# The last doubling level of a delta rule on one 64x64 block per head, with a longer latency in the scheduler for one small gather

## The chip, the core and the metric

The program runs on one core of a Trainium2 chip. The metric is device time in microseconds (us) of one execution. TensorE (PE in the profile, with PEld for its weight loads) does the matmuls and the transposes, VectorE (DVE), ScalarE (ACT) and GpSimd (POOL) the elementwise work, and SyncE (SP) issues nearly all DMAs. Each engine works through its own list of instructions in order and waits on semaphores for the others.

## The reference, cut to what matters

Two transformer blocks follow each other. The first mixes its 1024 tokens with a retention and with a gated delta rule of 4 heads, then runs a mixture of experts; the second has neighbourhood attention, a gated linear attention and an MLP. The change lies in the delta rule of the first block. With `C` the chunk length, it solves a unit lower triangular system in each chunk and carries a state from chunk to chunk:

```
a_mat = where(tri_strict, (k_beta @ k.T) * decay, 0)
t_mat = triangular_solve(eye + a_mat, eye, lower=True, unit_diagonal=True)
u = t_mat @ v_beta;  w = t_mat @ (k_beta * exp(g))
def step(state, inp):
    v_new = u_n - w_n @ state
    o_n = qg_n @ state + attn_n @ v_new
    state = state * gl_n + kt_n.T @ v_new
```

The kernel uses chunks of 128 tokens, so there are 8 of them, each with 4 heads and a 128x128 triangular matrix per head.

## The kernel before

**How work is ordered.** The program records every instruction as an object (all through one helper, which is why nearly every row of the profile names line 347), gives it a cost and a latency by a table, and then lists the instructions engine by engine: of those that are ready, the one with the largest sum of costs to the end of the program goes first. `load.lat`, which the change touches, is an addition to such an estimate; it alters no instruction, only the places where instructions stand.

**The delta rule.** `dn_pre(n)` makes, for chunk n, the matrix `dN` (the reference's `a_mat`, chunk rows on the partitions), its companions, and stores them (tensors `nb_d` and `pre_d`). `dn_blocks(s)` loads the 16x16 diagonal blocks of four chunks from `nb_d` into tile `N` (runs of 64 bytes), inverts them with 15 pairs of small VectorE steps, and stores the result to `xb_d`. `dn_scan(n)` builds the inverse of the whole matrix of a chunk by doubling: `Uf` holds the transposed inverse, `Ti` the inverse, first with 16x16 blocks only. At a level of block size b, GpSimd multiplies `dN` by a mask that keeps the blocks of size b under the diagonal (`AM`), four matmuls give `pp = AM.T @ Uf`, ScalarE copies that to `P`, four matmuls give `pu = Ti.T @ P`, VectorE subtracts it from `Uf`, and, but for the last level, four transposes and a VectorE copy make the new `Ti`. Levels are b = 16, 32, 64. Then the chunk's outputs and the state follow: a chain of matmuls with `vb`, `S` and `vn`. `mix_d` takes the result.

**What runs beside it.** `dn_chunks` records pre 0 to 3, blocks 0, scan 0, pre 4 and 5, scan 1, pre 6 and 7, blocks 1, scans 2 to 7. The scans are serial through the state. Between them on TensorE stand the filler, namely the projections of `tok_blocks` (128x512 matmuls in fp32r, a form of fp32 that takes one pass; each big product is three such), and the `retention` of the same tokens, 8 serial chunks whose single buffers make the load of one chunk wait for the end of the one before. After all this comes `mix_out`, from which on the order is the same in both kernels. A plain fp32 matmul of 128x128 shows as two TensorE records in the trace, a transpose as one.

The lines that matter: N's load (L1132), the VectorE steps (L1138 to L1144), the mask product (L1195), `pp` (L1199), the copy to `P` (L1201), `pu` (L1204), the subtraction (L1205), the transposes (L1209).

Of the kernel before, what the change touches and what calls it, by code (L numbers as in the profile page):

```python
# [15 lines left out]
AF = mybir.ActivationFunctionType  # L16
# [497 lines left out]
def shape_constants():  # L514
    i = np.arange(128)
    g = Cols()
    g.add('ident', np.eye(128))
    g.add('ones', np.ones((128, 128)))
    a = Cols()
    a.add('triU', i[:, None] <= i[None, :])  # L520
    a.add('bigN', BIG * (i[None, :] >= i[:, None]))
    a.add('negT', -BIG * (i[None, :] < i[:, None]))
    a.add('blk', i[:, None] // 16 == i[None, :] // 16)
    for b in (16, 32, 64):
        same = (i[:, None] // (2 * b)) == (i[None, :] // (2 * b))
        a.add(f'm{b}', same & ((i[:, None] // b) % 2 == 1) & ((i[None, :] // b) % 2 == 0))
    gam = 1.0 - 2.0 ** (-5.0 - np.arange(4.0))
    a.add('gq', gam[None, :] ** (i[:, None] + 1.0))
    a.add('gk', gam[None, :] ** (127.0 - i[:, None]) * 128.0 ** -0.5)
    a.add('rmask', (gam ** -128.0)[None, :, None] * (i[None, None, :] >= i[:, None, None]))  # L530
    a.add('invf', 10000.0 ** (-np.arange(0, 128, 2) / 128.0))
    m = Cols()
    m.add('strictU', i[:, None] < i[None, :])
    m.add('iota128', np.arange(128.0))
    m.add('iota64', np.arange(32.0) - 64.0)
    e32 = np.arange(32.0)
    kofs = -e32 - 2.0 ** 17 * (e32 < Kern.NS)
    m.add('kofs', np.concatenate([np.tile(kofs, (128, 1)), np.tile(kofs, 4)[:, None]], 1))
    m.add('ecol', np.tile(e32, 4)[:, None])
    m.add('iotaB', np.where(np.kron(np.eye(4), np.ones((32, 32))) > 0, np.tile(e32, 4), -1.0))  # L540
    m.add('tok', i[:, None] + 128.0 * np.arange(8)[None, :])
    w = Cols()
    cq, ck = i[:, None] % 64, np.arange(64)[None, :]
    cs = np.clip(cq - 8, 0, 48)
    w.add('colmask', np.where((ck >= cs) & (ck < cs + 16), 0.0, -BIG))
    l = Cols()
    l.add('m64', (i[:, None] % 64) > np.arange(64)[None, :])
    return {'k_g': g, 'k_a': a, 'k_m': m, 'k_n': w, 'k_l': l}, gam
# [14 lines left out]
class Kern:  # L563
# [564 lines left out]
    def dn_blocks(self, s):  # L1128

        nc, pd, V = self.nc, self.pd, self.nc.vector  # L1130
        N = self.t(pd, [128, 512], tag='P', bufs=2)[:, 0:256].rearrange("p (i j) -> p i j", j=16)
        nc.sync.dma_start(N, self.dram_ap(self.nb_d, 128 * 2064 * s, [[2064, 128], [128, 16], [1, 16]]))  # L1132
        X = self.t(pd, [128, 16, 2, 16], tag='AM', bufs=2)
        Y = self.t(pd, [128, 512], tag='P', bufs=2)[:, 0:256].rearrange("p (i j) -> p i j", j=16)
        flat = X.rearrange("p i t j -> p (i t j)")
        V.memset(flat, 0.0)
        V.memset(flat[:, 0:512:33], 1.0)
        for i in range(15):  # L1138
            r = [128, 15 - i, i + 1]
            y, x = Y[:, i + 1:, 0:i + 1], X[:, i + 1:, 0, 0:i + 1]  # L1140
            V.tensor_tensor(out=y, in0=N[:, i + 1:, i:i + 1].to_broadcast(r),
                            in1=X[:, i:i + 1, 0, 0:i + 1].to_broadcast(r), op=OP.mult)
            V.tensor_tensor(out=x, in0=x, in1=y, op=OP.subtract)
        V.tensor_copy(X[:, :, 1], X[:, :, 0].rearrange("p i j -> p j i"))  # L1144
        nc.sync.dma_start(self.xb_d[128 * s:128 * s + 128], flat)

    def dn_scan(self, A, n):
        nc, pd, sc = self.nc, self.pd, self.sc
        mm, tr = nc.tensor.matmul, nc.tensor.transpose
# [13 lines left out]
        kh, khT, dN, dT = [W[:, i] for i in range(4)]  # L1163
# [3 lines left out]
        Uf = self.t(pd, [128, 4, 128], tag='U', bufs=2)  # L1167
        Ti = self.t(pd, [128, 4, 128], tag='Ti', bufs=2)
        blk = A['blk'].rearrange("p (k j) -> p k j", j=16)[:, None].to_broadcast([128, 4, 8, 16])
        for eng, t, x in ((nc.gpsimd, 1, Uf), (nc.vector, 0, Ti)):  # L1170
            eng.tensor_tensor(out=x.rearrange("p h (k j) -> p h k j", j=16), in1=blk,
                              in0=C[:, :, t:t + 1, :].to_broadcast([128, 4, 8, 16]), op=OP.mult)
        for b in (16, 32, 64):
            AM = self.t(pd, [128, 4, 128], tag='AM', bufs=2)
            nc.gpsimd.tensor_tensor(out=AM, in0=dN, in1=A[f'm{b}'][:, None, :].to_broadcast([128, 4, 128]),
                                    op=OP.mult)
            pp = self.ps([128, 4, 128], 'dn')
            for h in range(4):
                mm(pp[:, h, :], AM[:, h, :], Uf[:, h, :], start=True, stop=True)
            P = self.t(pd, [128, 4, 128], tag='P', bufs=2)  # L1180
            nc.scalar.activation(P, pp, AF.Copy)
            pu = self.ps([128, 4, 128], 'dn')
            for h in range(4):
                mm(pu[:, h, :], Ti[:, h, :], P[:, h, :], start=True, stop=True)
            nc.vector.tensor_tensor(out=Uf, in0=Uf, in1=pu, op=OP.subtract)
            if b < 64:
                pt = self.ps([128, 4, 128], 'dn')
                for h in range(4):
                    tr(pt[:, h, :], Uf[:, h, :], self.ident)
                nc.vector.tensor_copy(Ti, pt)  # L1190
        pv = self.ps([128, 4, 128], 'tp')
        for h in range(4):
            tr(pv[:, h, :], lv_[:, h, :], self.ident)
# [1422 lines left out]
```

## Time and profile before

| | us |
|---|---|
| time, median of 3 runs | 2712.98 (2708.91 to 2715.82) |
| time of the profiled execution | 2710.75 |
| its span in the trace | 2708.9 |
| TensorE busy in it | 2529.4 (93%) |
| VectorE, ScalarE, GpSimd busy | 1801.0, 1194.9, 689.4 |

The span is what the trace covers; some 2 us of the time lie around it. Times of rows below are us from the span's start. The delta rule lies between about 190 and 612 us; all that the change reorders is between 190 and 640 us.

### The profile page before, as it was taken

The page shows a single profiled execution, that of the slowest core. Times are in us where ns is not written, and L with a number is a line of the kernel's source. Part 1 is how long each engine was busy: PE and PEld are TensorE (multiplying, and loading weights), DVE is VectorE, ACT ScalarE, POOL GpSimd, SP SyncE. Part 2 cuts the span into 40 slices and gives each one's busy share as a digit, 9 for nine tenths or more (in the row PEclk, how much of TensorE's full clock was granted, in tenths as well). Part 3 has the DMA queues.
Part 4 walks back from the last instruction along what each step waited for, and adds up shares of the span by engine and source line. Part 5 has one row for each costly group of instructions (what it writes and reads, how often), then busy time and mean ns, then how long its engine had stood idle before and what let it go on. Part 6 is the DMA issues. An engine that isn't in the chain of part 4 may idle for free. (4 is left out here: it accounts for less than half of the span.)

```text
span 2708.9 us, 35429 instructions
## 1 busy us (share of the span) xinstructions
PE 2529.4 (93%) x12278; PEld 1924.6 (71%) x12278; DVE 1801.0 (66%) x2583; ACT 1194.9 (44%) x2005; POOL 689.4 (25%) x703
## 2 busy tenths in 40 slices
PE   5999999999969999999996999999999999999998
PEld 4787777886657766454444777777787888887876
DVE  8557865546679889786776344358736767578874
ACT  5234332332236677565554434247714334453332
POOL 3006541422451111322234201144213003310002
PEclk9999999999979999999998999999999999999999
DMA  7238586565349999999978442263244768787473
GB/s 254 79 118 235 175 249 189 167 205 198 133 170 340 342 347 337 351 320 364 354 263 304 138 125 92 75 195 91 69 133 162 233 221 297 282 288 239 145 249 129
DMA packets 342100, 586.30 MB, mean 216 GB/s; under 512 B 74970, under 2 KB 112526, under 8 KB 338846
## 3 DMA queue, kind: packets, MB, share of 16 engines
q1 hardware_dynamic: 335262, 567.22, 62.6%
q0 software_dynamic: 6656, 16.79, 1.8%
q8 instruction: 97, 1.59, 0.2%
q14 instruction: 85, 0.70, 0.1%
HBM read 477.40 MB, written 112.41 MB: 218 GB/s over the span
## 5 line engine op out<-in xcount | busy, mean ns | idle before, releaser
L347 PE MATMUL psum_all<-sbuf 128*128 128x512 f32 (+10 forms) x12278 | 2529.4, 366 | 167.7 <-DVE sbuf L347 102.5
L347 PEld LDWEIGHTS psum_all<-sbuf 128*128 128x128 f32 (+6 forms) x12278 | 1924.6, 176 | 772.0 <-issue 158.9
L347 ACT ACTIVATE sbuf<-sbuf 128x1024 fp32r<-128x1024 f32 (+9 forms) x894 | 816.1, 937 | 769.9 <-PE psum_all L347 355.6
L347 DVE TENSOR_TENSOR sbuf<-sbuf,sbuf 128x1024 fp32r<-128x1024 f32 (+1 forms) x592 | 725.9, 1251 | 216.0 <-ACT sbuf L347 207.5
L347 ACT ACTIVATE sbuf<-psum_all 128x512 f32<-128x512 f32 (+12 forms) x742 | 345.9, 477 | 688.8 <-PE psum_all L347 636.6
L347 POOL TENSOR_TENSOR sbuf<-sbuf 128x512 f32<-128x512 f32 (+8 forms) x353 | 446.1, 1273 | 761.2 <-DVE sbuf L347 361.4
L347 DVE TENSOR_TENSOR sbuf<-sbuf 128x1024 f32<-128x1024 f32 (+12 forms) x417 | 316.4, 778 | 108.3 <-ACT sbuf L347 31.5
L347 DVE TENSOR_TENSOR sbuf<-psum_all,sbuf 128x512 f32<-128x512 f32 (+12 forms) x290 | 171.5, 603 | 157.7 <-ACT sbuf L347 71.4
L347 DVE SCALAR_TENSOR_TENSOR sbuf<-sbuf 128x512 f32<-128x512 f32 (+5 forms) x263 | 209.3, 803 | 46.3 <-POOL sbuf L347 36.9
L347 POOL TENSOR_SCALAR sbuf<-sbuf 128x1 f32<-128x1 f32 (+3 forms) x182 | 79.7, 440 | 627.0 <-ACT sbuf L347 491.9
L347 DVE TENSOR_TENSOR sbuf<-sbuf,psum_all 128x512 f32<-128x512 f32 (+6 forms) x191 | 123.5, 663 | 118.0 <-PE psum_all L347 112.7
L347 DVE TENSOR_SCALAR sbuf<-sbuf 128x32 f32<-128x32 f32 (+7 forms) x220 | 109.5, 510 | 60.9 <-ACT sbuf L347 42.0
L1809 POOL DMA_INDIRECT y_d<-sbuf x35 | 57.4, 1641 | 195.8 <-DVE sbuf L347 194.5
L347 DVE SCALAR_TENSOR_TENSOR sbuf<-sbuf,psum_all 128x128 f32<-128x128 f32 (+1 forms) x100 | 38.2, 411 | 84.9 <-PE psum_all L347 54.1
L1797 POOL DMA_INDIRECT sbuf<-h_d,sbuf x35 | 45.1, 1288 | 186.0 <-PE psum_all L347 153.1
L347 DVE SCALAR_TENSOR_TENSOR sbuf<-psum_all,sbuf 128x128 f32<-128x128 f32 (+9 forms) x109 | 62.0, 586 | 37.9 <-PE psum_all L347 37.4
L347 POOL MEMSET sbuf<- 64x64 f32 (+10 forms) x54 | 16.9, 314 | 193.4 <-DVE sbuf L347 114.9
L347 DVE CUSTOM_DVE_ANT_0 sbuf<-psum_all,sbuf 128x512 f32<-128x512 f32 (+2 forms) x80 | 48.1, 613 | 22.3 <-PE psum_all L347 21.8
L347 POOL TENSOR_TENSOR sbuf<-sbuf,sbuf 128x1024 fp32r<-128x1024 f32 x16 | 40.9, 2561 | 40.2 <-ACT sbuf L347 39.3
L347 ACT ACTIVATE sbuf<-psum_all,sbuf 128x128 f32<-128x128 f32 (+1 forms) x72 | 24.4, 402 | 35.5 <-PE psum_all L347 23.0
L347 DVE COPY sbuf<-psum_all 128x512 f32<-128x512 f32 (+9 forms) x39 | 20.6, 528 | 22.2 <-PE psum_all L347 19.0
L347 ACT ACTIVATION_READ_ACCUMULATOR sbuf<-sbuf 128x1 f32 x152 | 28.9, 190 | 0.0
(18 smaller groups left out, 112.3 us busy)
## 6 DMA issues: line engine op xcount, KB each, us to landing
sbuf<-in_w SPq DMA_DIRECT2D x384, 512.0 KB
sbuf<-in_w_ff SPq DMA_DIRECT2D x120, 512.0 KB
sbuf<-u_d SPq DMA_DIRECT2D x64, 512.0 KB
sbuf<-in_w_in SPq DMA_DIRECT2D x56, 512.0 KB
sbuf<-in_w_ada SPq DMA_DIRECT2D x48, 512.0 KB
u_d<-sbuf SPq DMA_DIRECT2D x64, 256.0 KB
sbuf<-in_x SPq DMA_DIRECT2D x16, 512.0 KB
sbuf<-qkv_d SPq DMA_DIRECT2D x32, 256.0 KB
```

The source lines that it names most:

```text
L347: op = self.new_op(eng, lambda: real(*a, **k), name, reads, writes)
L1797: return self.prog.real.gpsimd.indirect_dma_start(out=xg, out_offset=None, in_=self.h2_d, in_offset=bass.IndirectOffsetOnAxis(ap=tok, axis=0),
L1809: st = self.prog.real.gpsimd.indirect_dma_start(out=self.y_d, out_offset=bass.IndirectOffsetOnAxis(ap=dest, axis=0), in_=y, in_offset=None ...
```

## The change

It does the last level, b = 64, on the only block that this level has: rows 64 to 127 by columns 0 to 63 of each head. The mask `m64` and its product go. `pp` and `pu` become 64x64 matmuls that read 64 partitions (of `dN` directly, without mask), `P` and `Uf` are written only in that block, and as `Uf` is zero there before, the subtraction becomes a copy with factor -1 on ScalarE. And the load of `N` counts as 8000 ns longer in the scheduler's estimate.

```diff
-    for b in (16, 32, 64):
+    for b in (16, 32):
...
...
-        nc.sync.dma_start(N, self.dram_ap(self.nb_d, ...))
+        load = nc.sync.dma_start(N, self.dram_ap(self.nb_d, ...))
+        load.lat += 8000.0
...
-        for b in (16, 32, 64):
+        for b in (16, 32):
             AM = ...; pp = ...; P = ...; pu = ...
             nc.vector.tensor_tensor(out=Uf, in0=Uf, in1=pu, op=OP.subtract)
-            if b < 64:
-                pt = self.ps([128, 4, 128], 'dn')
-                for h in range(4):
-                    tr(pt[:, h, :], Uf[:, h, :], self.ident)
-                nc.vector.tensor_copy(Ti, pt)
+            pt = self.ps([128, 4, 128], 'dn')
+            for h in range(4):
+                tr(pt[:, h, :], Uf[:, h, :], self.ident)
+            nc.vector.tensor_copy(Ti, pt)
+
+        lo, up = slice(0, 64), slice(64, 128)
+        pp = self.ps([64, 4, 64], 'dn')
+        for h in range(4):
+            mm(pp[:, h, :], dN[up, h, lo], Uf[up, h, up], start=True, stop=True)
+        P = self.t(pd, [128, 4, 128], tag='P', bufs=2)
+        nc.scalar.activation(P[lo, :, lo], pp, AF.Copy)
+        pu = self.ps([64, 4, 64], 'dn')
+        for h in range(4):
+            mm(pu[:, h, :], Ti[lo, h, lo], P[lo, h, lo], start=True, stop=True)
+        nc.scalar.activation(Uf[lo, :, up], pu, AF.Copy, scale=-1.0)
```

In each of the 8 scans this takes away one GpSimd product of 128x512, eight fp32 matmuls of 128x128, one ScalarE copy of 128x512 and one VectorE subtraction of 128x512, and adds eight fp32 matmuls of 64x64 and two ScalarE copies of 64x256. The numbers of transposes and copies to `Ti` stay.

**TensorE, the last level of scan 6.** The rows are TensorE's in order; 128x128 are the delta rule's and the retention's matmuls and transposes, 128x512 the filler, and 64x64 the new matmuls. Before:

```order
L347 MATMUL psum_all<-sbuf_61 128x128 x4
L347 MATMUL psum_all<-sbuf_62 128x512
L347 MATMUL psum_all<-sbuf_61 128x128 x20
L347 MATMUL psum_all<-sbuf_62 128x512
L347 MATMUL psum_all<-sbuf_61 128x128 x8
L347 MATMUL psum_all<-sbuf_62 128x512 x5
```

The same place in the changed kernel:

```order
L347 MATMUL psum_all<-sbuf_62 128x512 x2
L347 MATMUL psum_all<-sbuf_61 64x64
L347 MATMUL psum_all<-sbuf_61 128x128
L347 MATMUL psum_all<-sbuf_61 64x64
L347 MATMUL psum_all<-sbuf_61 128x128 x2
L347 MATMUL psum_all<-sbuf_61 64x64
L347 MATMUL psum_all<-sbuf_61 128x128
L347 MATMUL psum_all<-sbuf_61 64x64
L347 MATMUL psum_all<-sbuf_62 128x512 x5
L347 MATMUL psum_all<-sbuf_61 64x64
```

The four `pp` no longer stand among matmuls of their own size; each is a single 64x64 between two of 128x128, here the transposes of the level before, which become ready at the same moment. Over the whole program the 64 new matmuls stand in 61 separate places: one group of four, and 60 single ones.

**VectorE, around the second `dn_blocks`.** Rows `128x15` and `128x14x2` are the first steps of the block inverse, `128x1024` are splits of weights for the filler, and `TENSOR_SCALAR` and `SCALAR_TENSOR_TENSOR` of 128x512 a product of the modulation vector. Before:

```order
L347 TENSOR_TENSOR sbuf_61<-psum_all,sbuf_61 128x512 x4
L347 TENSOR_TENSOR sbuf_62<-sbuf_61,sbuf_62 128x1024
L347 TENSOR_TENSOR sbuf_61<-sbuf_61 128x15
L347 TENSOR_TENSOR sbuf_62<-sbuf_61,sbuf_62 128x1024
L347 TENSOR_TENSOR sbuf_61<-sbuf_61 128x15
L347 TENSOR_TENSOR sbuf_62<-sbuf_61,sbuf_62 128x1024
L347 TENSOR_TENSOR sbuf_61<-sbuf_61 128x14x2 x2
```

Changed:

```order
L347 TENSOR_TENSOR sbuf_61<-psum_all,sbuf_61 128x512 x4
L347 TENSOR_TENSOR sbuf_62<-sbuf_61,sbuf_62 128x1024 x3
L347 TENSOR_TENSOR sbuf_61<-psum_all,sbuf_61 1x512
L347 TENSOR_SCALAR sbuf_61<-sbuf_61 128x512
L347 SCALAR_TENSOR_TENSOR sbuf_61<-sbuf_61 128x512
L347 SCALAR_TENSOR_TENSOR sbuf_61<-sbuf_61,psum_all 128x512
L347 SCALAR_TENSOR_TENSOR sbuf_61<-sbuf_61 128x512 x2
L347 TENSOR_TENSOR sbuf_61<-sbuf_61 128x15
L347 SCALAR_TENSOR_TENSOR sbuf_61<-sbuf_61 128x512
```

The first step moves behind the three weight splits and behind part of a modulation product, and the other 30 steps with it. On SyncE the store to `xb_d` follows: it stands 24 rows behind the load of `N` where it stood 17 behind it.

**TensorE, the end of the stage.** The long row of 128x512 is the filler between the last two chunks of the retention; 128x24 and 128x36 set up `mix_out`. Before:

```order
L347 MATMUL psum_all<-sbuf_61 128x128 x12
L347 MATMUL psum_all<-sbuf_62 128x512 x54
L347 MATMUL psum_all<-sbuf_61 128x128 x4
L347 MATMUL psum_all<-sbuf_62 128x512 x5
L347 MATMUL psum_all<-sbuf_61 128x128 x4
```

Changed:

```order
L347 MATMUL psum_all<-sbuf_61 128x128 x12
L347 MATMUL psum_all<-sbuf_62 128x512 x24
L347 MATMUL psum_all<-sbuf_61 128x24
L347 MATMUL psum_all<-sbuf_61 128x36 x8
L347 MATMUL psum_all<-sbuf_61 128x128 x28
```

The other filler has gone to earlier places: 24 instead of 54 stand before the last chunk of the retention, and none within it.

## Rows read from the trace of the kernel before

**Rows 1.** The page's first part (busy time and share of the span) and the head of its fourth (the chain of work that ended last, by engine).

```profile
PE 2529.4 (93%) x12278; PEld 1924.6 (71%) x12278; DVE 1801.0 (66%) x2583; ACT 1194.9 (44%) x2005; POOL 689.4 (25%) x703
...
PE 41%; DMA 3%; DVE 2%; issue 1%; POOL 1%; ACT 1%; POOLq 0%; SPq 0%; ACTq 0%; DVEq 0%
```

**Rows 2.** Stretches of the span: length, then busy time and number of records of each engine, the granted TensorE clock, the DMA share and GB/s.

```profile
190.00:263.00 73.00, 67.71 (x360) 54.56 (x358) 53.90 (x84) 39.00 (x121) 39.48 (x42) 1.00 0.78 235
263.00:295.00 32.00, 31.14 (x131) 24.88 (x132) 24.41 (x64) 8.08 (x27) 12.73 (x13) 0.95 0.78 236
295.00:350.00 55.00, 49.74 (x274) 39.73 (x273) 43.80 (x55) 20.44 (x64) 35.15 (x31) 0.97 0.56 177
350.00:405.00 55.00, 50.88 (x303) 43.15 (x304) 32.03 (x53) 20.71 (x66) 21.17 (x22) 1.00 0.81 239
405.00:440.00 35.00, 31.36 (x147) 23.02 (x147) 24.39 (x57) 5.13 (x8) 1.28 (x1) 1.00 0.90 255
440.00:480.00 40.00, 39.16 (x278) 36.59 (x279) 20.88 (x49) 12.52 (x43) 11.60 (x13) 0.96 0.46 141
480.00:520.00 40.00, 38.01 (x265) 34.00 (x264) 23.54 (x40) 13.43 (x32) 15.62 (x15) 1.00 0.50 169
520.00:560.00 40.00, 39.95 (x292) 36.92 (x291) 22.46 (x53) 15.24 (x47) 13.86 (x18) 1.00 0.41 139
560.00:612.00 52.00, 48.12 (x306) 42.13 (x304) 25.01 (x41) 16.44 (x48) 16.46 (x16) 1.00 0.71 237
```

**Rows 3.** TensorE's own timeline, the places where it sat idle before a stretch of work: start, length, the first instruction of the stretch, number of records, and in brackets the idle time before it and what ended that.

```profile
263.86 32.25 PE L347 MATMUL psum_all<-sbuf 128*128 128x128 f32 x135 [3.12 <-ACT sbuf L347]
298.24 4.60 PE L347 MATMUL psum_all<-sbuf 128*128 128x128 f32 x27 [2.13 <-POOL sbuf L347]
327.50 18.01 PE L347 MATMUL psum_all<-sbuf 128*128 128x128 f32 x87 [2.05 <-POOL sbuf L347]
392.05 11.83 PE L347 MATMUL psum_all<-sbuf 128*128 128x128 f32 x65 [2.69 <-DVE sbuf L347]
440.84 69.88 PE L347 MATMUL psum_all<-sbuf 128*128 128x128 f32 x489 [2.92 <-DMA sbuf<-rq_d]
516.10 46.14 PE L347 MATMUL psum_all<-sbuf 128*128 128x128 f32 x332 [0.96 <-DMA sbuf<-rq_d]
600.56 10.37 PE L347 MATMUL psum_all<-sbuf 128*128 128x128 f32 x61 [1.24 <-DMA sbuf<-rq_d]
614.21 2.08 PE L347 MATMUL psum_all<-sbuf 128*128 128x36 f32 x14 [3.28 <-DVE sbuf L347]
617.16 4.10 PE L347 MATMUL psum_all<-sbuf 128*128 128x128 f32 x14 [0.86 <-DVE sbuf L347]
```

**Rows 4.** Two short stretches of TensorE alone: in the first all records are fp32 of 128x128, in the second all are 128x512.

```profile
470.30:478.10 7.80, 7.80 (x72) 1.00 0.52 167
278.00:295.00 17.00, 17.00 (x76) 1.00 0.59 187
```

**Rows 5.** The weight loads' timeline in a later stage of the kernel, where single fp32 matmuls with a stationary tile of 128x64 and of 128x128 follow each other directly, each with two records and 128 columns. Start, length, form and number of records, idle before.

```profile
1730.98 0.19 PEld L347 LDWEIGHTS psum_all<-sbuf 128*64 128x64 f32 x2 [0.35 <-issue]
1731.34 0.20 PEld L347 LDWEIGHTS psum_all<-sbuf 128*128 128x128 f32 x2 [0.17 <-issue]
1731.71 0.63 PEld L347 LDWEIGHTS psum_all<-sbuf 128*64 128x64 f32 x10 [0.17 <-issue]
```

**Rows 6.** The same view elsewhere: four transposes of 64x64, one record each, behind other forms.

```profile
1104.72 0.32 PEld L347 LDWEIGHTS psum_all<-sbuf 64*128 64x128 f32 x4 [0.36 <-issue]
```

**Rows 7.** Groups by form between 440 and 612 us: number, busy time and mean ns of one, idle before and its releasers; the last row, from the same view of the whole span, is a copy of 64x256.

```profile
L347 POOL TENSOR_TENSOR sbuf<-sbuf 128x512 f32<-128x512 f32 x30 | 39.3, 1328 | 72.6 <-PE psum_all L347 53.5 <-DVE sbuf L347 15.4 <-DMA sbuf<-pre_d 3.5
L347 ACT ACTIVATE sbuf<-psum_all 128x512 f32<-128x512 f32 x50 | 29.5, 597 | 80.9 <-PE psum_all L347 80.7
L347 DVE TENSOR_TENSOR sbuf<-sbuf,psum_all 128x512 f32<-128x512 f32 x22 | 15.1, 686 | 30.4 <-PE psum_all L347 30.3
...
L347 ACT ACTIVATE sbuf<-psum_all 64x256 f32<-64x256 f32 x16 | 5.8, 373 | 1.9 <-PE psum_all L347 1.9
```

**Rows 8.** The block inverse on VectorE's timeline: the first steps of `dn_blocks` 0, then the first steps of `dn_blocks` 1, three rows of modulation and weight work near it, and its last copy.

```profile
271.40 2.57 DVE L347 TENSOR_TENSOR sbuf<-sbuf 128x15 f32<-128x15 f32 x11
...
403.43 0.18 DVE L347 TENSOR_TENSOR sbuf<-sbuf 128x15 f32<-128x15 f32 x1
...
416.10 0.68 DVE L347 SCALAR_TENSOR_TENSOR sbuf<-sbuf,psum_all 128x512 f32<-128x512 f32 x1
...
423.44 0.37 DVE L347 COPY sbuf<-sbuf 128x256 f32<-128x256 f32 x1
...
432.82 1.23 DVE L347 TENSOR_TENSOR sbuf<-sbuf,sbuf 128x1024 fp32r<-128x1024 f32 x1 [1.93 <-ACT sbuf L347]
```

**Rows 9.** SyncE's issues (start, length, transfer) around `dn_blocks` 1: the load of `N`, the store to `xb_d`, the next loads of it.

```profile
399.33 0.37 SPq L347 DMA_DIRECT2D sbuf<-nb_d  x1
...
423.96 0.47 SPq L347 DMA_DIRECT2D xb_d<-sbuf  x1
...
428.95 0.92 SPq L347 DMA_DIRECT2D sbuf<-xb_d  x2
```

**Rows 10.** GpSimd's longest wait between 398 and 432 us: waited for, total us, times, longest.

```profile
POOL sbuf L347 <- DMA xb_d<-sbuf: 29.7, 1, 29.7
```

**Rows 11.** SyncE's issues at the end of the stage.

```profile
592.11 0.32 SPq L347 DMA_DIRECT2D zg_d<-sbuf  x1
595.89 0.32 SPq L347 DMA_DIRECT2D sbuf<-mod_d  x1
596.46 0.32 SPq L347 DMA_DIRECT2D sbuf<-rq_d  x1
```

More of the change, by code (lines that the diff above doesn't have):

```diff
@@ L1131, in dn_blocks @@
         N = self.t(pd, [128, 512], tag='P', bufs=2)[:, 0:256].rearrange("p (i j) -> p i j", j=16)
-        nc.sync.dma_start(N, self.dram_ap(self.nb_d, 128 * 2064 * s, [[2064, 128], [128, 16], [1, 16]]))
+        load = nc.sync.dma_start(N, self.dram_ap(self.nb_d, 128 * 2064 * s, [[2064, 128], [128, 16], [1, 16]]))
+        load.lat += 8000.0
         X = self.t(pd, [128, 16, 2, 16], tag='AM', bufs=2)
```

## The prediction, made before the changed kernel ran

> **What bounds the kernel now.** The first part of the page and the chain of waits come first: TensorE is busy for 93% of the span and stands ahead of every other engine in the chain that ended last [rows 1]. Shares over a whole span say nothing of one stage, so the stretches of the stage come next [rows 2]. They show two kinds. From 440 to 560 us TensorE is busy 117.1 of 120 us and VectorE, ScalarE and GpSimd at most 59% of any row: here a microsecond of TensorE work is a microsecond of time. Up to 440 us TensorE idles more, 19 us in 250; and its timeline names who it waited for: GpSimd at 298.24 and 327.50, VectorE at 392.05, the retention's load of q at 440.84 [rows 3]. There, work taken from GpSimd or VectorE can pay, and TensorE work can hide. At the stage's end TensorE waits again, for the load of the retention's last q and then for VectorE [rows 3]. So the question is what the change does to TensorE's own time first, and to these few waits second.
>
> **TensorE work removed.** Eight fp32 matmuls of 128x128 in each of 8 scans, 64 in all, two records each. A stretch of such records alone shows 72 in 7.80 us, of which one is cut by the edge: 0.11 us each [rows 4]. 64 x 2 x 0.11 = 14.1 us go.
>
> **TensorE work added.** 64 fp32 matmuls of 64x64, again two records each. No such matmul is in the trace. Their bare records are bounded by four 64x64 transposes in 0.32 us, 0.08 each [rows 6], and by half of 0.11, since half as many columns stream; I take 0.07, 128 x 0.07 = 9.0 us (7.0 to 10.2). Were that all, TensorE would win 5 us. But the order puts the 64 matmuls in 61 separate places between 128-wide ones, and the trace has that case. Single matmuls with stationary tiles of 128x64 and 128x128 follow each other at 1730.98, 1731.34 and 1731.71, that is 0.36 and 0.37 us each [rows 5], against 2 x 0.11 = 0.22 for two such records in a row. Nothing holds them (the idle before each is marked as issue): a change of the tile's size costs about 0.145 us, on the way in and on the way out. With only 64 columns to finish the way out should be cheaper by half a record, 0.05, so I put 0.24 on each separate place: 61 x 0.24 = 14.6 us. Bounds: 61 x 0.29 = 17.7 us, and nothing, if a 64x64 tile differs from the 128x64 one of those rows. Sum: 9.0 + 14.6 - 14.1 = +9.5 us, between 7.0 - 14.1 = -7.1 and 17.7 + 10.2 - 14.1 = +13.8. Between these ends I stay by the row on alternating tiles, which is the same pattern on the same engine.
>
> The Trainium skill has two rules here that pull apart, both on the page TensorEngine Tiling (Array Packing). Its section Theoretical Speedup gives a matmul with one small dimension up to twice the throughput, and with two small ones more; by that the added 9.0 us would at most be halved or quartered, and with nothing for the separate places the time is that of the second rival below. Its section Key Properties says "Mode switching requires drain", which speaks against the change, since the order switches 122 times; it names no price. The trace agrees with the second, with 0.36 us where 0.22 would do; no run here shows two tiles at work at once.
>
> **The other engines' share of the level.** GpSimd loses one 128x512 product per scan, 8 x 1.33 = 10.6 us, VectorE one subtraction, 8 x 0.69 = 5.5 us; ScalarE exchanges a 0.60 us copy for two of 0.37, 8 x 0.15 = +1.2 us [rows 7]. After 440 us all of this lies beside TensorE, which is the bound, and is worth nothing by itself; the cover is the filler, and where that is gone the chain of one scan gets 0.69 + 0.60 - 2 x 0.37 = 0.55 us shorter. Only scans 0 and 1 run where TensorE waits for GpSimd and VectorE. Their two 1.33 us products may shorten the two waits of 2.13 and 2.05 us, but the order still places other products of the same size ahead, and a TensorE wait at 440.84 is for a load that does not move. The same place hides a part of two scans' added TensorE work, 2/8 of 9.5 = 2.4 us at most. I put -1 us on both together, between -11 (the waits at 298.24, 327.50, 392.05 and 440.84 sum to 9.8, and 1 us of shorter chains) and +2.
>
> **The 8000 ns.** They are a belief of the scheduler, not a wait. The load of N was never late: the first VectorE step of blocks 0 at 271.40 and of blocks 1 at 403.43 have no idle time before them [rows 8]. So nothing is gained there, and the 31 steps stand later. In blocks 1 the first step now stands behind modulation steps that ran until about 416.1, 12.5 us later than 403.43; the end stands behind a split of weights that ran at 432.82, where the last copy had started at 423.44 [rows 8], some 10 us later. Behind that copy is the store to `xb_d` at 423.96 on SyncE, and behind it the loads at 428.95 [rows 9]; behind the loads GpSimd waits, for 29.7 us already [rows 10], and scans 2 to 7. While they wait TensorE does filler, which the order has pulled forward. So the delay costs nothing at once; it costs filler, and the bill comes at the end.
>
> **The end of the stage.** Between retention chunks 6 and 7 lies a round trip of a store and the load of q at 596.46 [rows 11], and chunk 7 starts at 600.56 after 1.24 us of idle [rows 3]. Now 54 matmuls of 128x512 fill it, at 17.00 us for 75, 0.227 each [rows 4], 12.2 us. In the changed order 24 stand there, 5.4 us, and the set-up of `mix_out`, about 2.1 us by the row at 614.21 [rows 3]: 12.2 - 7.5 = 4.7 us of new idle. Chunk 7 itself has lost its filler too; its stretch took 10.37 us, of which 28 filler matmuls were 6.4, and I reckon that some 3 us of that turn into idle. On the other side the waits at 614.21 and 617.16, 3.28 + 0.86 = 4.1 us [rows 3], lose their reason, as that set-up is done by then. 4.7 + 3 - 4.1 = 3.6; as the filler that left fills a little idle earlier, I take +3 us (0 to +10, the upper end if the 4.1 us stay and the scans end late).
>
> **The sum**, against the profiled execution's 2710.75 us: +9.5 - 1 + 3 = +11.5, that is 2722.3. The median of before lies 2.2 us above that execution, so the same sum on it gives 2724.5. I predict 2723.
>
> **Rivals.**
> *The filler runs out in earnest.* The scans start 10 us later and each is longer on TensorE, so scan 7, which is the last before `mix_out`, ends after the retention with nothing beside it. For it: only 24 filler matmuls stand at the end. Against it: the period of a scan is set by TensorE, and less of the other filler lies between them now, so the scans may run faster one after the other. Price: the 10 us of the late start unhidden in place of 3, 2723 + 8 = 2731 to 2735.
> *A 64x64 tile does not have to wait for a change of size.* Then TensorE's sum is -7.1 to -4 us. With -1 and +3 the time is 2705.7 to 2708.8, and with no cost at the end down to 2702: this rival is on the other side, not slower. It decides from a switch cost below 0.04 us per way, at which 61 x 0.08 = 5 us equals the gain in bare records. For it: no row has a 64x64 fp32 matmul beside a 128x128 one. Against it: the 128x64 rows [rows 5], and 0.36 us of idle marked issue ahead of the 64x64 transposes [rows 6].
> *The early waits go.* With less work on GpSimd and VectorE and with filler pulled forward, the waits before 440 us vanish, up to 9.8 us of them: 2723 - 10 = 2713, no change. For it: GpSimd is busy 35 of 55 us between 295 and 350 [rows 2]. Against it: only two of its 31 instructions there go.
> *The switches come and the other terms too, but the change of latency does nothing.* It is part of the forecast: without the +3 the sum is 2719 to 2721.
>
> **How the numbers follow.** About 0.3% of this time, 8 us, is what a measurement of this kernel can tell from no change. Forecast (2716 to 2729) 0.58; filler runs out 0.14; no switch cost 0.10; early waits go 0.18. Slower by over 0.3% means above 2721: 0.39 of the forecast and all of the first rival, 0.53. Within: the rest of the forecast, 0.19, most of the third and half of the second rival, 0.39. Faster: 0.08. The range takes in the third rival, most of the first, and part of the second: 2704 to 2734.
>
> **What would show it.** In the changed kernel's weight loads each single 64x64 should start some 0.35 to 0.4 us before the next 128-wide load of its neighbour, with idle marked issue on both sides; TensorE's records between 190 and 640 us should be about as many, and the stretch longer. The wait of GpSimd for `xb_d` should last some 10 us longer, with TensorE busy meanwhile. Ahead of retention chunk 7 TensorE should be idle some 6 us, not 1.24. It would be wrong if the 64x64 matmuls follow at 0.11 us a record or less, or if TensorE's idle before 440 us, 19 us now, falls by half.

## The result and the profile after

The changed kernel took 2727.56 us in the median of 4 runs, the kernel before 2711.18 in the median of 4: a ratio of 1.0067, with a 95% interval of 1.0054 to 1.008. In a later comparison it was 1.0061 (1.0047 to 1.0075). It is slower, by some 16 us. The first part of its page, against [rows 1]:

```profile
PE 2546.1 (93%) x12278; PEld 1930.1 (71%) x12278; DVE 1792.1 (66%) x2575; ACT 1196.1 (44%) x2013; POOL 675.4 (25%) x695
```

TensorE is busy for 16.7 us more with the same number of records, while VectorE and GpSimd do less, as the change says. TensorE's own idle places in the stretch that was reordered answer to [rows 3]:

```profile
263.46 37.90 PE L347 MATMUL psum_all<-sbuf 128*128 128x128 f32 x157 [2.79 <-ACT sbuf L347]
302.18 4.58 PE L347 MATMUL psum_all<-sbuf 128*128 128x128 f32 x27 [0.81 <-POOL sbuf L347]
308.80 21.39 PE L347 MATMUL psum_all<-sbuf 128*128 128x128 f32 x126 [2.04 <-DVE sbuf L347]
385.28 21.83 PE L347 MATMUL psum_all<-sbuf 128*128 128x128 f32 x101 [1.88 <-ACT sbuf L347]
443.30 58.42 PE L347 MATMUL psum_all<-sbuf 128*128 128x128 f32 x376 [3.43 <-DMA sbuf<-rq_d]
556.15 59.98 PE L347 MATMUL psum_all<-sbuf 128*128 128x128 f32 x395 [2.00 <-POOL sbuf L347]
618.18 3.47 PE L347 MATMUL psum_all<-sbuf 128*128 128x36 f32 x16 [2.04 <-DVE sbuf L347]
628.35 1.12 PE L347 MATMUL psum_all<-sbuf 128*128 128x128 f32 x4 [6.70 <-DMA sbuf<-rq_d]
630.15 1.11 PE L347 MATMUL psum_all<-sbuf 128*128 128x128 f32 x4 [0.69 <-ACT sbuf L347]
631.95 2.07 PE L347 MATMUL psum_all<-sbuf 128*128 128x128 f32 x8 [0.69 <-ACT sbuf L347]
634.88 4.82 PE L347 MATMUL psum_all<-sbuf 128*128 128x128 f32 x24 [0.85 <-DVE sbuf L347]
...
666.34 15.65 PE L347 MATMUL psum_all<-sbuf 128*128 128x32 f32 x81 [0.34 <-DVE sbuf L347]
```

The last row is the first one of the router's matmuls, from where both kernels run alike; before, the same row starts at 649.12. So all of the loss, 17.2 us, lies ahead of it. Its place is read from two stretches of each trace, which end at that row: the whole stage from one and the same record at some 225 us, and the last 60 us. The columns are length, TensorE's busy time and records, the granted clock as a mean, the DMA share, GB/s. Before:

```profile
224.63:649.12 424.49, 396.51 (x2326) 0.98 0.66 204
589.12:649.12 60.00, 53.58 (x255) 0.91 0.73 249
618.00:624.00 6.00, 5.57 (x18) 0.50 0.96 327
624.00:630.00 6.00, 6.00 (x24) 0.86 0.78 267
630.00:640.00 10.00, 9.73 (x55) 1.00 0.40 107
```

After:

```profile
224.56:666.34 441.78, 410.24 (x2326) 0.96 0.63 196
606.34:666.34 60.00, 47.99 (x243) 0.83 0.74 261
...
618.00:624.00 6.00, 3.47 (x16) 0.53 1.05 414
624.00:630.00 6.00, 1.12 (x4) 0.50 1.01 383
630.00:640.00 10.00, 8.00 (x36) 0.56 0.77 268
```

What a stretch gives can be split in three: waits (its length less TensorE's busy time), work at full clock (busy time times granted clock) and what the lower clock takes (the rest). As TensorE waits most where the clock is low, the product of the two means of a long stretch overstates the loss; below, each stretch is cut into pieces of 0.25 us and the products are added up. The last 60 us then hold 6.4 us of waits and 4.5 us of lower clock before, 12.0 and 5.8 after: the end of the stage loses 17.8 us instead of 10.9. Nearly all of the difference is waiting. The granted clock stands at its lower level, 1.2 GHz, for longer: in both kernels it is there (0.50, 0.53) from 618 to 624 us, behind the first waits; but from 630 to 640 us it was 1.00, the upper level of 2.4 GHz, before, and is 0.56 after, behind the wait of 6.70 us. But from 618 to 630 us, where it is low in both, only 4.6 us of work stand after, against 11.6 before, so the lower clock costs just 1.3 us more in all.

The whole stage splits the same way: 386.9 us of work at full clock, 28.0 of waits and 9.6 of lower clock before, 397.7, 31.5 and 12.6 after. Of the 17.3 us, TensorE's work is 10.8, waits are 3.5 and the lower clock is 3.0.

### The profile page after: what moved, and what is told of

Read it like the earlier page. It is cut to its first block, busy times and chain, and to the rows that moved or that the text cites. A ratio compares the mean times of both kernels' runs of the same rounds, so it can differ in the third digit from the quotient of the medians.

```text
span 2725.8 us, 35451 instructions
## 1 busy us (share of the span) xinstructions
PE 2546.1 (93%) x12278; PEld 1930.1 (71%) x12278; DVE 1792.1 (66%) x2575; ACT 1196.1 (44%) x2013; POOL 675.4 (25%) x695
## 5 line engine op out<-in xcount | busy, mean ns | idle before, releaser
L347 PE MATMUL psum_all<-sbuf 128*128 128x512 f32 (+11 forms) x12278 | 2546.1, 367 | 167.3 <-DVE sbuf L347 99.2
L347 PEld LDWEIGHTS psum_all<-sbuf 128*128 128x128 f32 (+7 forms) x12278 | 1930.1, 176 | 782.9 <-issue 165.8
L347 ACT ACTIVATE sbuf<-psum_all 128x512 f32<-128x512 f32 (+13 forms) x750 | 346.7, 473 | 714.9 <-PE psum_all L347 647.4
L347 POOL TENSOR_TENSOR sbuf<-sbuf 128x512 f32<-128x512 f32 (+7 forms) x345 | 430.1, 1255 | 797.4 <-DVE sbuf L347 388.7
L347 DVE TENSOR_TENSOR sbuf<-sbuf 128x1024 f32<-128x1024 f32 (+13 forms) x417 | 313.7, 771 | 115.7 <-ACT sbuf L347 32.5
```

Of the source, the lines that this page charges most:

```text
L347: op = self.new_op(eng, lambda: real(*a, **k), name, reads, writes)
```

## The experiments

Every comparison is with the kernel before on the same chip. "Work at full clock" and "lost at the end" (waits + lower clock, in the last 60 us of the stage) are split as above, each from one profiled execution; "filler" is the number of 128x512 matmuls between the last two retention chunks, and within the last, in TensorE's order. In the two kernels with a separate buffer for the retention's result (own buffer), the retention ends ahead of the last scans, so the filler says nothing of the end, and the start of the stage is found by the number of TensorE's records.

| kernel | ratio to before (95%) | stage, us | TensorE busy in it | work at full clock | lost at the end | filler |
|---|---|---|---|---|---|---|
| before | 1 | 424.5 | 396.5 | 386.9 | 6.4 + 4.5 | 54 + 16 |
| changed | 1.0067 (1.0054 to 1.008) | 441.8 | 410.2 | 397.7 | 12.0 + 5.8 | 24 + 0 |
| changed, again | 1.0061 (1.0047 to 1.0075) | 444.1 | 410.0 | 398.1 | 13.5 + 5.1 | 24 + 0 |
| level alone | 1.0015 (1.0002 to 1.0028) | 427.6 | 403.8 | 397.2 | 4.5 + 3.1 | 54 + 16 |
| 8000 ns alone | 0.9993 (0.998 to 1.0006) | 424.1 | 395.2 | 385.7 | 5.4 + 1.6 | 53 + 9 |
| level, 2000 ns | 1.0034 (1.0021 to 1.0047) | 432.5 | 406.5 | 396.3 | 4.9 + 2.1 | 61 + 10 |
| level, 4000 ns | 1.0041 (1.0025 to 1.0057) | 437.8 | 407.1 | 396.6 | 5.6 + 1.7 | 54 + 0 |
| level, 16000 ns | 1.0079 (1.0066 to 1.0092) | 452.2 | 417.7 | 396.6 | 18.6 + 5.7 | 9 + 0 |
| changed, own buffer | 1.004 (1.0025 to 1.0056) | 433.0 | 403.1 | 397.9 | 6.4 + 2.0 | 11 + 12 |
| changed, 64x64 in groups | 1.0032 (1.0021 to 1.0044) | 426.1 | 392.8 | 383.1 | 9.0 + 4.9 | 43 + 0 |
| grouped, no latency | 1.0003 (0.9991 to 1.0015) | 423.5 | 394.2 | 382.5 | 9.8 + 3.2 | 58 + 16 |
| grouped, no latency, own buffer | 0.9983 (0.9974 to 0.9992) | 424.7 | 391.6 | 383.5 | 7.7 + 3.0 | 12 + 15 |
| changed, wide tile | 0.9994 (0.9983 to 1.0005) | 422.4 | 394.8 | 384.6 | 6.5 + 5.1 | 40 + 0 |
| wide tile, no latency | 0.9983 (0.9973 to 0.9994) | 419.1 | 389.8 | 387.1 | 8.0 + 2.6 | 47 + 16 |

The work at full clock sorts the kernels by the form of the last level alone, whatever the order: 396.3 to 398.1 us in the seven with single 64x64 matmuls, 382.5 to 383.5 in the three with groups, 384.6 and 387.1 with the wide tile, 385.7 and 386.9 without the change.

**The two parts alone.** One kernel has the narrow last level without the added latency:

```diff
-        load.lat += 8000.0
```

> The narrow last level without the 8000 ns: 64 matmuls of 64x64 stand again singly among 128-wide ones, and the first dn_blocks steps stand where they stood. Theory (the changes of tile size cost TensorE some 13 us net, the longer latency some 5 us at the end of the stage): 8 to 13 us above the kernel before, 2719 to 2724 us, with no idle above 2 us ahead of the last retention chunk. Rival (the latency and the order that it makes are what costs): within 4 us of the kernel before.

Measured: 2715.29 against 2710.63 us, 1.0015 (1.0002 to 1.0028). The other is the kernel before with that line alone.

> The kernel before with the 8000 ns alone. Theory: TensorE's work is unchanged, so only waits move: some 3 us less before 440 us, some 3 to 8 us more at the end of the stage, sum 0 to +6 us, 2711 to 2717 us. Rival (the latency is what costs): 10 to 18 us above the kernel before.

Measured: 2709.57 us, 0.9993 (0.998 to 1.0006): no difference. The level alone costs 4 to 5 us, neither the 8 to 13 of the theory nor clearly the rival's nothing, and the latency alone costs nothing, just below the theory's range; both together cost 16. TensorE's idle places in the kernel with the level alone say in part why it costs less than its matmuls do:

```profile
299.23 4.61 PE L347 MATMUL psum_all<-sbuf 128*128 128x128 f32 x27 [1.52 <-POOL sbuf L347]
326.44 2.08 PE L347 MATMUL psum_all<-sbuf 128*128 128x128 f32 x12 [0.57 <-POOL sbuf L347]
...
390.60 11.80 PE L347 MATMUL psum_all<-sbuf 128*128 128x128 f32 x65 [1.18 <-DVE sbuf L347]
...
442.24 38.28 PE L347 MATMUL psum_all<-sbuf 128*128 128x128 f32 x265 [1.69 <-DMA sbuf<-rq_d]
...
608.84 9.93 PE L347 MATMUL psum_all<-sbuf 128*128 128x128 f32 x59 [0.66 <-DMA sbuf<-rq_d]
622.04 18.34 PE L347 MATMUL psum_all<-sbuf 128*128 128x36 f32 x83 [3.27 <-DVE sbuf L347]
```

Four waits of 2.13, 2.05, 2.69 and 2.92 us in [rows 3] are down to 1.52, 0.57, 1.18 and 1.69, 4.8 us less, and the last retention chunk has its filler and waits 0.66 us. Over the stage of the profiled execution, 10.3 us more work stand against 4.1 us less waiting and 3.0 us less lower clock.

**The switches of tile size.** In the changed kernel the four `pp` and the four `pu` of a level were made to stand together by a higher place in the scheduler's list:

```diff
-            mm(pp[:, h, :], dN[up, h, lo], Uf[up, h, up], start=True, stop=True)
+            op = mm(pp[:, h, :], dN[up, h, lo], Uf[up, h, up], start=True, stop=True)
+            op.base += 1e6
 # the same for pu
```

> The changed kernel, in which the 64 matmuls of 64x64 stand in 16 groups of four instead of 61 places, by a higher place in the scheduler's list; the same instructions otherwise. Theory (each separate place costs 0.24 to 0.3 us): 45 places fewer are 11 to 14 us less than the changed kernel, 2713 to 2717 us. Rival (a 64x64 matmul is slow by itself, or the rest of the change costs): within 4 us of the changed kernel, 2724 to 2730 us.

Measured: 2718.3 us, 1.0032 (1.0021 to 1.0044), some 9 us below the changed kernel: 0.0035 in the ratios; a little short of what was expected. TensorE's busy time in the stage fell from 410.2 to 392.8 us, and its work at full clock by 14.6 us, which is 0.32 us for each of the 45 places. By form, from 190 to 640 us in the changed kernel, and from 260 to 640 us in the grouped one, which are all the 64x64 matmuls in both:

```profile
L347 PE MATMUL psum_all<-sbuf 64*64 64x64 f32 x128 | 20.2, 241 | 0.0
```

```profile
L347 PE MATMUL psum_all<-sbuf 64*64 64x64 f32 x128 | 10.8, 224 | 0.0
```

The same 128 records take half the time when four matmuls stand together; the rest of the 14.6 us shows in the records beside them. A second way keeps the stationary tile at 128x128 and streams only the 64 columns; the rows that should not count meet zeros or are not read:

```diff
-            mm(pp[:, h, :], dN[up, h, lo], Uf[up, h, up], start=True, stop=True)
+            op = mm(pp[:, h, :], dN[:, h, :], Uf[:, h, up], start=True, stop=True)
+            op.cost = 135.0
-        nc.scalar.activation(P[lo, :, lo], pp, AF.Copy)
+        nc.scalar.activation(P[:, :, lo], pp, AF.Copy)
...
-            mm(pu[:, h, :], Ti[lo, h, lo], P[lo, h, lo], start=True, stop=True)
+            op = mm(pu[:, h, :], Ti[:, h, :], P[:, h, lo], start=True, stop=True)
+            op.cost = 135.0
-        nc.scalar.activation(Uf[lo, :, up], pu, AF.Copy, scale=-1.0)
+        nc.scalar.activation(Uf[lo, :, up], pu[lo], AF.Copy, scale=-1.0)
```

Left out (`...`) are `pp` and `pu`, which become 128 partitions wide. The edit also sets the scheduler's estimate for such a matmul to 135 ns, where a narrow one has 270, so the order differs too.

> The changed kernel, in which the last level's matmuls keep a stationary tile of 128x128 and stream 64 columns (the other half of the rows is zero or not used), so that no tile size changes; mask product and subtraction stay removed, the latency stays. Theory: 128 records at 0.06 to 0.07 us in place of 0.11 gain 5 us on TensorE, waits -3 and the end of the stage +5: 2703 to 2711 us. Rival (records of 64 columns cost as much as those of 128, or the loss is not in the tile size): 2714 us or more.

Measured: 2709.16 us, 0.9994 (0.9983 to 1.0005), some 18 us below the changed kernel, and within the theory's range, but not for its reason. Against the kernel before, TensorE's work fell by 2.3 us and not by 5, and 87 of the 128 records of 64 columns are followed by the next record only 0.11 us later, as the rival said. Of the 19.4 us between the stages of the changed and the wide kernel, 13.1 are TensorE's work, and 6.2 are waits and lower clock at the end of the stage, where the new order has more filler (40 instead of 24).

> The last level with a stationary tile of 128x128 and 64 columns, without the 8000 ns. Theory (no change of tile size, TensorE 2 to 5 us less, filler left at the end of the stage as in the kernel before): 3 to 8 us below the kernel before. Rival (the latency helps, as it hides the gather): slower than the same kernel with the 8000 ns.

Measured: 2707.12 against 2712.85 us, 0.9983 (0.9973 to 0.9994). That is faster than both kernels, by 0.17%. It is not clearly faster than the wide kernel with the latency, as the two intervals overlap; a gain by the latency is not seen. TensorE's work is that of the kernel before (387.1 against 386.9 us), so the 0.17% do not come from it; in the profiled execution the lower clock takes 2.6 us of the stage instead of 9.6, and what causes that was not tried. The groups and the wide tile together show that the narrow tile standing singly among wide ones is what costs TensorE, and that the rest of the change (one product, one subtraction less) is harmless or a small gain.

**The end of the stage.** The changed kernel ran again beside the next three.

> The changed kernel as it is, beside the others on one chip. Theory (narrow level and latency together cost more than the sum of each alone): 14 to 20 us above the kernel before. Rival (the first comparison was of unlike chips or runs): 2 to 8 us above the kernel before, the sum of the two parts alone.

Measured: 2728.64 against 2712.85 us, 1.0061: the sum of the parts alone is not what both together cost.

The size of the latency was varied:

```diff
-        load.lat += 8000.0
+        load.lat += 4000.0      # then 2000.0 and 16000.0
```

> The changed kernel with 4000 ns in place of 8000 ns. In its order 54 filler matmuls stand between the last two retention chunks, where the changed kernel has 24. Theory (what the latency costs is filler that is missing there): 30 more are 6.8 us, which take the wait for q away and hold the clock, 6 to 11 us below the changed kernel. Rival (the latency costs by the delay of the block inverse, or by nothing that the order shows): within 4 us of the changed kernel, or half way to the kernel without latency.

Measured: 2723.88 us, 1.0041 (1.0025 to 1.0057), 5 us below the changed kernel, between the two expectations. The place is right: lost at the end are 7.3 us instead of 17.8 or 18.6. But about half of that came back elsewhere in the stage.

> The changed kernel with 2000 ns. In its order 61 filler matmuls stand between the last two retention chunks and 10 within the last. Theory: the end of the stage costs no more than in the kernel with the level alone, so 8 to 13 us below the changed kernel, 2715 to 2720 us. Rival (the loss grows with the latency itself): a quarter of the way from the level alone to the changed kernel, 2718 to 2721 us, with the loss ahead of 440 us.

Measured: 2720.8 us, 1.0034 (1.0021 to 1.0047). That is outside the theory's range and inside the rival's, but not in the rival's place. Again the end lost little (7.0 us), and again the time is above the level alone, by 5 us, which the filler at the end does not explain. The traces show one place: from 440 to 480 us, around and behind the wait for the retention's q, TensorE loses 1.7 us in the level alone and 8.4 us with 2000 as with 4000 ns. The rows are those of the level alone, of 2000, of 4000 and of 8000 ns with the level, and the last of 8000 ns alone:

```profile
440.00:480.00 40.00, 38.31 (x268) 1.00 0.50 157
440.00:480.00 40.00, 36.32 (x217) 0.87 0.41 116
440.00:480.00 40.00, 34.41 (x202) 0.91 0.53 147
440.00:480.00 40.00, 36.70 (x229) 0.96 0.40 127
440.00:480.00 40.00, 37.03 (x233) 0.87 0.42 126
```

The 8000 ns alone lose 7.6 us there, 5.1 more than the kernel before, but win most of it back at the end. These are single executions.

> The changed kernel with 16000 ns. In its order 9 filler matmuls stand between the last two retention chunks, 15 fewer than in the changed kernel. Theory (missing filler there is idle time): 15 x 0.227 = 3.4 us more idle ahead of the last chunk, 2 to 6 us above the changed kernel. Rival (the filler there does not decide): within 2 us, or below.

Measured: 2733.09 us, 1.0079 (1.0066 to 1.0092), 3 to 5 us above the changed kernel by the ratios, within the theory's 2 to 6. Its last rows, beside those of the changed kernel above:

```profile
626.15 3.63 PE L347 MATMUL psum_all<-sbuf 128*128 128x36 f32 x16 [5.99 <-DVE sbuf L347]
636.97 1.12 PE L347 MATMUL psum_all<-sbuf 128*128 128x128 f32 x4 [7.19 <-DMA sbuf<-rq_d]
638.77 1.11 PE L347 MATMUL psum_all<-sbuf 128*128 128x128 f32 x4 [0.69 <-ACT sbuf L347]
640.57 2.07 PE L347 MATMUL psum_all<-sbuf 128*128 128x128 f32 x8 [0.69 <-ACT sbuf L347]
...
649.41 1.20 PE L347 MATMUL psum_all<-sbuf 128*128 128x512 f32 x4 [1.32 <-ACT sbuf L347]
```

With 9 filler matmuls left the set-up of `mix_out` comes too early as well and waits 5.99 us: 2.04 + 6.70 have become 5.99 + 7.19, 4.4 us more. Most of that stands ahead of the set-up and not, as the theory had it, ahead of the last chunk. The loss at the end is 24.3 us, of which the lower clock is 5.7, no more than in the changed kernel.

**Another buffer for the retention's result.** The result of a chunk shares its buffer with the next chunk's q, which is why the load of q waits for a store:

```diff
-            zt = self.t(pd, [128, 512], tag='rq', bufs=1)
+            zt = self.t(pd, [128, 512], tag='rz', bufs=1)
```

> The changed kernel, in which the retention writes its result into a buffer of its own, so that the load of q for the next chunk need not wait for the store; the scheduler then finishes the retention long before the last scan. Theory (on top of TensorE's 11 us, the rest comes from the last retention chunk that runs alone at the end of the stage, with idle time and a low granted clock): 8 to 14 us below the changed kernel, 2714 to 2720 us. Rival (the rest comes from the late start of scans 2 to 7 itself): within 4 us of the changed kernel, as the scans start no earlier.

Measured: 2722.98 us, 1.004 (1.0025 to 1.0056), 6 us below the changed kernel, short of the 8 to 14. The loss at the end fell from 18.6 to 8.4 us, and the stage of the profiled execution is 11 us shorter than that of the changed kernel beside it; the medians show half of it. The part after the stage, which no edit touches, took between 2053.8 and 2062.3 us in the profiled executions, so a single execution is not to be read to better than some microseconds.

**Looking for more.** The grouped level without latency, and the same with the buffer:

> The narrow last level with its 64x64 matmuls in 16 groups of four, without the 8000 ns. Theory (in groups the level takes some 4 us from TensorE, and 58 filler matmuls stand between the last two retention chunks, so no loss at the end): 4 to 10 us below the kernel before. Rival (any 64x64 matmul costs, or the level's gain is only waits): within 3 us of the kernel before.

Measured: 2709.61 us, 1.0003 (0.9991 to 1.0015). The expectation failed. TensorE's work did fall by 4.4 us, but over the stage 1.4 us of waits and 2.1 of lower clock came in its place, and the end loses 13.0 us instead of 10.9, with no less filler than before (58 + 16).

> The same with the retention's result in a buffer of its own. Theory (the wait of the last retention chunk for its q is gone altogether): 0 to 5 us below the grouped kernel without latency. Rival (retention early only moves the wait to the last scan, which then runs alone): 0 to 6 us above it.

Measured: 2707.94 us, 0.9983 (0.9974 to 0.9992), as fast as the wide tile without latency. So two kernels beat both that were compared.

## Why the prediction was right, point by point

**The direction and the size.** Forecast were +11.5 us and 2723 us; it became 2727.56, inside the range, and slower by over 0.3%. The range, 2704 to 2734, also took in no change, so lying inside it says little; what follows goes by the terms. Forecast were +9.5 of TensorE's work, -1 and +3 of waits, and nothing for the clock; measured in the profiled executions are +10.8, +3.5 in all and +3.0.

**TensorE's work: right, from two terms that were off against each other.** Forecast was 0.24 us for each separate place and +9.5 us in all; the work at full clock grew by 10.8. The load track of the changed kernel, in the last level of scan 6, whose order stands with the change above, answers to [rows 5]:

```profile
569.87 0.97 PEld L347 LDWEIGHTS psum_all<-sbuf 64*64 64x64 f32 x7 [0.36 <-issue]
571.01 1.76 PEld L347 LDWEIGHTS psum_all<-sbuf 64*64 64x64 f32 x10 [0.17 <-issue]
573.14 1.90 PEld L347 LDWEIGHTS psum_all<-sbuf 64*64 64x64 f32 x12 [0.37 <-issue]
```

From the first `pp` at 569.87 to the first `pu` at 573.14 stand, by the order, four 64x64 matmuls, four transposes and five filler matmuls. The latter nine cost 4 x 0.11 + 5 x 0.227 = 1.58 us, which leaves 1.69 for the four, 0.42 each. The prediction had 0.24 + 2 x 0.07 = 0.38. 61 x 0.42, and some 0.1 for each of the three others, are 26 us; less 14.1, some +12 by this one place, where the whole stage shows +10.8. The bare records were put too high: in a group of four, as at 506.41 us in the grouped kernel, the loads of 64x64 follow each other in 0.058 us, not 0.07 (and the four transposes of [rows 6], whose stationary tile is 64x128, also start 0.06 us apart, as the 0.32 us hold the last one's full length). The price of a place was put too low: 0.42 - 2 x 0.058 is 0.30, and the groups gave 0.32, not 0.24. As forecast, the longer idle times before single ones are marked issue; but a single 64x64 starts 0.26 us before the next 128-wide load, as from 569.87 to 570.13, and not the 0.35 to 0.4 that were to show it. The Trainium skill says on the page TensorEngine Tiling (Array Packing), section Key Properties, that changing the tiling mode drains TensorE. These rows agree in that a switch costs time, 0.30 us here; that it is a drain they do not show. The gain that the section Theoretical Speedup of that page of the Trainium skill gives is not seen here, as 128 records took 20.2 us, 0.158 each, against 0.11 for the larger ones that they replaced.

**Waits ahead of 440 us: right in sign.** Forecast -1, with a rival of -10. TensorE's idle time from 190 us to the retention's q at 440.84 was 20.0 us before; after, up to the same point at 443.30, it is 17.2: -2.9 us. The stretches, before and after:

```profile
190.00:260.74 70.74, 67.71 (x360) 1.00 0.77 232
260.74:440.84 180.10, 163.12 (x855) 0.98 0.75 223
```

```profile
190.00:260.67 70.67, 68.38 (x363) 1.00 0.77 232
260.67:443.30 182.63, 167.76 (x853) 0.98 0.74 222
```

In the level alone the four waits that the rival named lost 4.8. So this rival was true in part and hides in the sum.

**The end of the stage: right in place, too small.** Forecast were 4.7 + 3 - 4.1, taken as +3. The idle time ahead of the last chunk is 6.70 us (forecast 5.9), inside the chunk 0.69 + 0.69 + 0.85 + 0.44 = 2.7 (forecast 3), and the wait for the set-up is still 2.04 of the 4.1 that were to go. Over the last 60 us that is 5.6 us more waiting (12.0 against 6.4), not 3, mostly because the wait for the set-up did not go. The granted clock, which the prediction put at nothing, adds 1.3 us there, and 3.0 over the whole stage; with it the end loses 6.9 us more than before.

**The 8000 ns: half wrong.** That they gain nothing is right: alone they change nothing, and the steps of the block inverse moved as forecast. First step and last copy of the second block inverse in the changed kernel, and GpSimd's longest wait, against [rows 8, 10]:

```profile
416.67 0.18 DVE L347 TENSOR_TENSOR sbuf<-sbuf 128x15 f32<-128x15 f32 x1
...
436.45 0.38 DVE L347 COPY sbuf<-sbuf 128x256 f32<-128x256 f32 x1
```

```profile
POOL sbuf L347 <- DMA xb_d<-sbuf: 42.9, 1, 42.9
```

Both are 13 us later, and GpSimd waits 13 us longer. The prediction priced the latency as a term of its own (+3) that would be there with or without the other part, and a kernel without it at 2719 to 2721. It is not such a term: alone it costs nothing, and 53 filler matmuls stay at the end; with the narrow level it costs 12 to 14 us. In the profiled executions 7.6 us of that are waits, nearly all of them at the end, and 6.0 are lower clock, of which 2.7 at the end. That the end depends on filler agrees with the kernels with 0, 8000 and 16000 ns, of which the filler falls (54, 24, 9) and the loss at the end rises (7.6, 17.8, 24.3), and with 2000 and 4000 ns, where filler and loss stay as with 0. It is not the filler alone: the grouped kernel without latency has 58 and loses 13.0. What stays open is the middle: with 2000 and 4000 ns the end loses no more than with the level alone and the kernel is still 5 to 7 us slower. The traces place most of that between 440 and 480 us; why the latency moves waits there, and why the scheduler leaves less filler with both parts than with either, was not tried.

## What to carry to other kernels

Half of the arithmetic on a smaller tile is no gain when that tile stands singly among full ones: count the places at which the tile's size changes in the engine's order and price each, here at 0.3 us, before counting the work. Either put the small matmuls side by side, or keep the stationary tile and let zeros do the masking, which gave the removal of the mask product without the price. And when an estimate of a latency moves work in a list schedule, look at what it leaves for the last serial chain: filler that is gone there came back as idle time, 5.6 us here. Price the lower clock behind such a wait by the work that stands in that time; here it took 1.3 us more.

## What the runs showed of the hardware that was not expected

Streaming half the columns saved little by itself. In the grouped kernel 128 records with a stationary tile of 64x64 took 10.8 us, while in the kernel with the wide tile and no latency the 128 records with 128x128 stationary and 64 columns took

```profile
L347 PE MATMUL psum_all<-sbuf 128*128 128x64 f32 x128 | 17.9, 261 | 0.1
```

The 17.9 us hold some time in which these records overlap with others; one starts 0.11 us after the other in most cases, the same as records of 128 columns. Where the kernel before has fp32 matmuls of 128x128 only, the load track is busy all the time, as the stretch of [rows 4] shows for it:

```profile
470.30:478.10 7.80, 7.80 (x71) 1.00 0.52 167
```

That is one load of 128x128 per record, each 0.11 us behind the other. It is the same in the wide kernel without latency, where eight records of 64 columns stand in a row and the load track has no idle time either:

```profile
459.75:460.56 0.81, 0.81 (x9) 1.00 0.15 56
```

So the loads may set the pace there, and not the columns that stream. That is argued, not shown: the two loads of 128x128 at 1731.34 in [rows 5] start only 0.06 us apart. Within a group of four the records of 64x64 follow each other in 0.058 us, so there the smaller stationary tile does save time.
